# Sliding attention's queries and keys, made with channels on partitions and scored 32 rows at a time

## The chip, the cores and the metric

The kernel runs on one core of a Trainium2 chip. The metric is the device time of one execution in microseconds; of the kernel before there are three runs, and one further execution with the hardware profiler on. Lower is better.

## What is computed

A trunk of two layers over one sequence of 256 tokens with 1024 channels. Each layer normalises its input, multiplies it by one wide matrix `w_in` (1024 by 12,832 columns), and cuts the product into the inputs of three token mixers and of their gates: a state-space scan (branch A), sliding-window attention (branch B) and forgetting attention (branch C). The three results are projected, weighted by sigmoid gates, summed, projected once more and added to the stream. The change is in branch B:

```
q = rope(q.reshape(b, s, 16, 64), cos, sin)      # 16 query heads of 64 channels
k = rope(k.reshape(b, s, 4, 64), cos, sin)       # 4 key heads, each for 4 query heads
scores = einsum('bnqkgd,bnskd->bnkgqs', qb, kb) * 64 ** -0.5
# a query sees itself and the 127 tokens before it; each head has a sink logit
probs = softmax(concat([masked scores, sink]))[..., :-1]
out = einsum('bnkgqs,bnskd->bnqkgd', probs, vb) * silu(z)

def rope(x, cos, sin):                            # x1, x2: channels 0..31 and 32..63 of a head
    return concatenate([x1 * c - x2 * s, x2 * c + x1 * s], axis=-1)
```

All values are float32.

## The kernel before

*Products.* A float32 product with weights is made of three products in the type `F32R`: weights and activations are split into a high part and a low rest, and high times high, low times high and high times low are accumulated. Weights come from HBM in pieces of 256 to 512 columns, each cut into parts of 1024 values per partition (`load_part`, DMAs on SP's queue, six buffers). ACT writes a part's high half, DVE its low half (`split`, L258 to L265; `feed`, L353), at most four parts ahead of their use (`AHEAD`), into six buffers. A piece takes 8 blocks of contraction times 3 terms = 24 products for each of two halves. There are two forms. `tok` (L445) has tokens on partitions: 128 tokens are stationary, the piece's columns are the moving operand, once for each block t of 128 tokens. `chan` (L438) has channels on partitions: 128 columns of the piece are stationary, all 256 tokens move. Products stream their moving operand "in turn" (columns i and n/2 + i alternating); the pieces of 272 columns alone are streamed in plain order (`turn=False`).

*Branch B, before.* Queries and keys are made by `tok`. `rope` (L463) multiplies the product by the cosine and sine rows with three DVE instructions, POOL adds the two results (L495, L519), then PE transposes them by the identity (L101) and ACT writes the transposed blocks out (L490, L503, L528): 2 transposes for each block of queries (`u_bq`), 4 for each block of keys (`u_bkv`). So a head's 64 channels lie on one half of the partitions, and two heads stand on top of each other. `swa_quad` scores a group of four heads: 8 products that contract 64 rows, two heads side by side on the two row halves, into four PSUM tiles of their own. Products like these are in plain float32, and each leaves two records in the trace.

*The quad.* `attn_quad` (L534) is shared with forgetting attention: scores on PE, a fused add and minimum on DVE (L561), exponentials on ACT (L567), scaling on DVE (L579), 12 transposes on PE, evictions on ACT (L596), products with the values on PE.

*What sets the order.* PE's order is written out by the program. The heavy work is a list of operations (`ops`), each one half of a piece. Between two of them `pump` enters waiting pieces of the light work (quads, scan groups, norms, transposes) when their due time has come on a clock that adds up estimated costs of PE instructions; a generator's `yield D_...` is the time until its next part is due, a yielded name or condition holds it until a token or a state is there. `drain` forces what is left. On DVE, ACT and POOL a scheduler orders by priority, but in the first stage of layer 0 the program's order stands there as well.

*Layer 0's start.* To begin early, the first pieces are multiplied with activations that aren't normalised, and the products are scaled by 1/rms afterwards (`y.rn`, for rope by scaled tables, L1306). In the meantime `normalize` (L1164) spreads 1/rms over partitions by two products with `ones`, scales the transposed activations (L1178, four DVE instructions) and splits them again. Channel-form products can come only after that. Before, this stage holds keys, values, all queries, the step sizes of the scan (`C_DT`, in a piece of 272 columns with queries) and a value piece of branch C (352 columns); those of branch C were cut to 352, 344 and 344 columns and hold its forget logits too.

*Layer 1's start.* The normalised activations of token block 0 are there earlier than those of block 1, so the first operations are in token form on block 0: keys and values as one piece of 512, and queries of 256.

Of the kernel before, what the change touches and what calls it, by code (L numbers as in the profile page):

```python
# [44 lines left out]
def hybrid_trunk(  # L45
# [45 lines left out]
    def mm(o, a, b, **kw):  # L91
        n = b.free_size()
        if a.dtype == F32R:
            clock["t"] += max(0.094, n / 2350.0)
        else:
            clock["t"] += max(0.2, n / 587.0) * (0.5 if a.free_size() == 64 else 1.0)
        nc.tensor.matmul(o, a, b, **kw)  # L97
# [90 lines left out]
    rope_sb = T("rope", [P, 2, 2, 64])  # L188
# [113 lines left out]

    subs = []
# [91 lines left out]
    def load_rope(queue):  # L395
        queue.dma_start(rope_sb, rope_tab.rearrange("(t p) c d -> p t c d", p=P))

    def layer_consts(y, queue):
        l = y.l
        pdma = pin(queue.dma_start)  # L400
        if l:
            load_rope(queue)
# [60 lines left out]
    def rope(y, p, t):  # L463

        p4 = p.rearrange("p a (h d) -> p a h d", h=2)
        a = T("L1", [P, 4, 64])
        b = T("L1", [P, 4, 64])
        a4, b4 = (v.rearrange("p (a h) d -> p a h d", a=2) for v in (a, b))
        for o, i, r in ((a4, p4, rope_sb[:, t, 0, :]),
                        (b4[:, :, :, 0:32], p4[:, :, :, 32:64], rope_sb[:, t, 1, 0:32]),  # L470
                        (b4[:, :, :, 32:64], p4[:, :, :, 0:32], rope_sb[:, t, 1, 32:64])):
            tt(o, i, bc(bc(r, 1, 2), 1, 2), op=ALU.mult)
        return a, b

    def u_bkv(y, c0, t, placed=None):


        def f(w):
            p = tok(y.hTh, y.hTl, w, t) if placed is None else ordered(placed[t][:, 0:w.n])
            if t == 0 and c0 == 0:  # L480
                kv = T("L8", [P, 2048])
                y.kT = kv[:, 0:1024].rearrange("p (h s) -> p h s", h=4)
                y.bv = kv[:, 1024:1536].rearrange("p (t c) -> p t c", t=2)
            (late.append if placed is not None else lambda g: g())(lambda: evict(w, p))

        def evict(w, p):
            if c0 > 0:
                act(halves(y.bv[:, t, :]), p, AF.Copy, scale=y.rn[:, t:t + 1])
            elif w.n == 512:
                act(y.bv[:, t, :], p[:, 1, :], AF.Copy)  # L490
            if c0 == 0:
                a, b = rope(y, p if w.n == 256 else halves(p[:, 0, :]), t)
                kd = T("L2", [P, 4, 2, 64])
                for i in range(2):
                    gtt(kd[:, :, i, :], a, b, op=ALU.add)  # L495
                launch(1, rest(kd), D_K if y.rn is None else 2 * D_K)
            pump()

        def rest(kd):
            pt = pmx()  # L500
            for h in range(4):
                transpose(pt[:, h * P:(h + 1) * P], kd[:, h, :, :].rearrange("p a b -> p (a b)"), ident)
            act(y.kT[:, :, t * P:(t + 1) * P], pt.rearrange("p (h s) -> p h s", h=4), AF.Copy)  # L503
            yield 0.0
        return f

    def u_bq(y, c0, t, mid=None):

        def f(w):
            p = tok(y.hTh, y.hTl, w, t, turn=w.n != 272, mid=mid)  # L510
            if w.n == 272:
                logits(y, t, 0, p[:, 0:16])
                p = halves(p[:, 16:272])
            for i in range(w.n // 256):
                if t == 0:
                    y.qT[c0 + i] = T("qt", [P, 2, S])
# [345 lines left out]
    def fox_quad(y, j):  # L862
# [17 lines left out]
        def scored():  # L880
            tokens["bias"] += 1
# [468 lines left out]
```

## Time and profile before

| | |
|---|---|
| median of 3 runs (lowest, highest) | 839.42 us (839.38, 839.81) |
| the profiled execution's own time | 839.45 us |
| its span, first to last instruction | 837.7 us |
| granted TensorE clock, mean | 0.999 |
| HBM read, written | 154.76 MB, 2.16 MB |
| instructions | 16280 |

The page of the profile gives busy times of the engines (PE is TensorE's products, PEld its weight loads, DVE VectorE, ACT ScalarE, POOL GpSimd, SP the queue that issues the weights), the span in 40 slices, the chain of work that ended last, and groups of instructions. A group's name is what it writes, an arrow, and what it reads: `mm<-L,hi` is a product into PSUM tile `mm` with activations `L` moving over stationary weights `hi`. Rows of a group end with a count, the busy time, the mean length in ns, and the idle time ahead of it with its cause.

### The profile page before, as it was taken

To read this page: it belongs to the slowest core of one execution; us is meant where nothing else is said; L and a number is where in the kernel's file an instruction comes from. 1 tells how busy PE (TensorE), PEld (TensorE's weight loads), DVE (VectorE), ACT (ScalarE), POOL (GpSimd) and SP (SyncE) were. 2 spreads that over 40 slices of the span, in tenths; PEclk is the share of its full clock that TensorE was granted. 3 is DMA by queue.
4 is the path that set the end of the run, shared out by engine and by line. 5 is a ranking of instruction groups with operands and counts; after the bars stand their busy time and mean duration, and the time that the engine had idled before them with its cause. 6 is when DMAs were issued, how large, how long until landed. Compare 5 with 4: busy or idle time off the path is not lost.

```text
span 837.7 us, 16280 instructions
## 1 busy us (share of the span) xinstructions
PE 828.7 (99%) x6067; PEld 767.2 (92%) x6067; DVE 650.2 (78%) x1426; ACT 510.9 (61%) x1022; POOL 102.3 (12%) x141
## 2 busy tenths in 40 slices
PE   8999999999999999999999999999999999999996
PEld 8999999989999998888999999999899999988896
DVE  6987898998766679665787688899968667785665
ACT  7477768665666657443654676876557567654442
POOL 1810000000221010220024000100003110121000
PEclk9999999999999999999999999999999999999999
DMA  9775467676565556665676544765756564476632
GB/s 307 220 216 169 119 185 229 204 214 203 153 198 176 153 165 203 207 221 186 211 247 213 152 121 147 226 216 187 247 175 183 155 189 151 153 238 214 214 101 76
DMA packets 123113, 157.99 MB, mean 189 GB/s; under 512 B 5746, under 2 KB 90090, under 8 KB 123034
## 3 DMA queue, kind: packets, MB, share of 16 engines
q1 hardware_dynamic: 108816, 140.53, 53.6%
q10 hardware_dynamic: 13962, 16.37, 6.2%
q8 instruction: 48, 0.79, 0.4%
q14 instruction: 31, 0.25, 0.1%
q0 software_dynamic: 256, 0.05, 0.0%
HBM read 154.76 MB, written 2.16 MB: 187 GB/s over the span
## 4 chain that ended last, share of the span: by engine, by line
PE 98%; DMA 1%; DVE 0%; SPq 0%; POOLq 0%; issue 0%; ACT 0%
PE mm L97 84%; PE mx L97 9%; PE mx L101 4%; DMA L<-in_x_dram 1%; SPq L330 0%; SPq L164 0%; DVE L L1214 0%; POOLq L1346 0%; ACT L L1028 0%; DVE L L1222 0%; DVE L L1003 0%; DVE L L1007 0%; DVE sm L230 0%; DVE rs L232 0%; DVE sm L256 0%
## 5 line engine op out<-in xcount | busy, mean ns | idle before, releaser
L262 DVE TENSOR_TENSOR lo<-raw,hi 128x1024 fp32r<-128x1024 f32 (+3 forms) x262 | 312.7, 1208 | 85.8 <-ACT hi L261 75.4
L97 PE MATMUL mm<-hi,L 128*128 128x512 f32 (+4 forms) x1424 | 376.5, 352 | 0.2
L97 PE MATMUL mm<-L,hi 128*128 128x256 f32 x1792 | 318.0, 279 | 0.0
L261 ACT ACTIVATE hi<-raw 128x1024 fp32r<-128x1024 f32 (+3 forms) x262 | 264.1, 1022 | 84.7 <-PE mm L97 76.6
L97 PEld LDWEIGHTS mm<-L,hi 128*128 128x128 f32 x1792 | 277.9, 192 | 7.4 <-issue 3.9
L97 PEld LDWEIGHTS mm<-hi,L 128*128 128x128 f32 x1424 | 251.0, 190 | 26.3 <-issue 2.1
L97 PE MATMUL mm<-lo,L 128*128 128x512 f32 (+4 forms) x712 | 247.1, 348 | 0.0
L97 PE MATMUL mm<-L,lo 128*128 128x256 f32 x896 | 246.7, 275 | 0.0
L97 PEld LDWEIGHTS mm<-L,lo 128*128 128x128 f32 x896 | 172.1, 192 | 0.2
L97 PEld LDWEIGHTS mm<-lo,L 128*128 128x128 f32 x712 | 134.6, 190 | 12.3
L874 POOL TENSOR_SCALAR_AFFINE_SELECT bias<-bias 128x128 f32<-128x128 f32 x64 | 34.1, 569 | 409.5 <-DMA bias<-cumd 291.1
L567 ACT ACTIVATE pp<-pp,nm 128x128 f32<-128x128 f32 (+1 forms) x128 | 56.6, 444 | 13.2 <-DVE nm L561 11.2
L696 DVE SCALAR_TENSOR_TENSOR L<-L,vec,L 128x255 f32<-128x255 f32 (+2 forms) x96 | 46.1, 481 | 2.1 <-ACT L L693 1.1
L699 ACT ACTIVATE L<-L 128x256 f32<-128x256 f32 x32 | 13.3, 417 | 41.1 <-DVE L L696 41.1
L898 ACT ACTIVATE L<-L 128x512 f32<-128x512 f32 x24 | 15.2, 631 | 36.5 <-DVE L L897 36.3
L97 PE MATMUL mx<-L,L 128*64 128x128 f32 (+1 forms) x384 | 34.5, 314 | 0.0
L579 DVE TENSOR_SCALAR pp<-pp,rsum 128x128 f32<-128x128 f32 (+1 forms) x128 | 32.3, 317 | 0.3
L780 ACT ACTIVATE L<-mm 128x256 f32<-128x256 f32 x48 | 18.1, 378 | 20.5 <-PE mm L97 20.5
L97 PEld LDWEIGHTS mx<-L,L 128*64 128x64 f32 x384 | 22.9, 136 | 8.3 <-issue 1.4
L596 ACT ACTIVATE L<-mx 128x512 f32<-128x512 f32 x48 | 26.8, 596 | 1.2 <-PE mx L101 1.0
L101 PE MATMUL mx<-ident,pp 128*128 128x128 f32 x192 | 26.3, 273 | 0.0
L897 DVE TENSOR_TENSOR L<-mm,L 128x512 f32<-128x512 f32 x24 | 16.5, 687 | 12.3 <-PE mm L97 12.3
(187 smaller groups left out, 726.6 us busy)
## 6 DMA issues: line engine op xcount, KB each, us to landing
raw<-in_w_in_dram SPq DMA_DIRECT2D x179, 512.0 KB, 4.6
raw<-in_w_proj_dram SPq DMA_DIRECT2D x48, 512.0 KB, 4.5
raw<-in_w_out_dram SPq DMA_DIRECT2D x16, 512.0 KB, 4.8
raw<-in_w_in_dram SPq DMA_DIRECT2D x16, 344.0 KB, 3.2
L<-cumd ACTq DMA_DIRECT2D x8, 512.0 KB, 5.0
bias<-cumd ACTq DMA_DIRECT2D x16, 256.0 KB, 3.6
L<-in_gate_bias_dram ACTq DMA_DIRECT2D x12, 256.0 KB, 5.2
raw<-in_w_in_dram SPq DMA_DIRECT2D x8, 352.0 KB, 3.3
```

Source lines behind the costliest of these rows:

```text
L97: nc.tensor.matmul(o, a, b, **kw)
L101: nc.tensor.transpose(o, a, i)
L261: keep(act)(hi, src, AF.Copy)
L262: keep(tt)(lo, src, hi.bitcast(F32), op=ALU.subtract)
L567: act(pp[:, i, sl], pp[:, i, sl], AF.Exp, scale=-1.0, bias=nm[:, e:e + 1], accum_out=sums[:, e:e + 1])
L579: ts(pp[:, i, sl], pp[:, i, sl], rs[:, 2 * i + b:2 * i + b + 1], 0.5, op0=ALU.mult, op1=ALU.mult)
L596: act(pT, pt, AF.Copy)
L696: stt(a[:, s:S], x_[:, 0:S - s], y.vec[:, 16 * j + u:16 * j + u + 1], a[:, s:S], op0=ALU.mult, op1=ALU.add)
L780: act(halves(th), p, AF.Tanh, scale=0.5)
L874: nc.gpsimd.affine_select(out=bias[:, i, dst], in_=bias[:, i, src], compare_op=ALU.is_ge, fill=NEG, base=0, pattern=[[-1, P]], channel_mul ...
L897: tt(halves(g), p, halves(y.gb), op=ALU.add)
L898: act(g, g, AF.Tanh, scale=0.5)
```

## The change

- Queries and keys are made by `chan`, so they come out with channels on partitions, and nothing is transposed. Their weights' columns are reordered when they are split: of four heads, the first 32 channels of each fill the first 128 columns, the other 32 the second (`turned`, in `feed`). The split of such a part is two instructions on each engine instead of one.
- The cosine and sine tables are turned once by PE at the start (`tables`, two transposes, eight ACT copies). Each half of the product is multiplied by both on DVE (`rotated`), and POOL adds and subtracts (`add_rotated`).
- A head's two channel halves lie on the same 32 rows. The keys, made once, are shifted by 32, 64 and 96 rows with six SBUF-to-SBUF DMAs from POOL's queue, so that each query head finds its key head on its own row quarter.
- Scores are 16 products of 32 rows: for each query block and each channel half, four heads on the four row quarters, accumulated over the two channel halves.
- The pieces' order and widths change. Layer 0 starts with values and two 256-column value pieces of branch C; layer 1 with branch C's values (512) and the values. Then keys and four query groups in channel form. The step sizes and the forget logits move into two pieces of 272 columns with branch C's values, which are streamed in turn; the decay logits follow the second.
- The first sliding quad waits for the first gate piece in layer 0 too; the values lie in a `bias` buffer.

```diff
@@ mm @@
-            clock["t"] += max(0.2, n / 587.0) * (0.5 if a.free_size() == 64 else 1.0)
+            clock["t"] += max(0.2, n / 587.0) * (0.5 if a.free_size() == 64 or a.shape[0] == 32 else 1.0)
@@ feed @@
-            split(hi, lo, raw, keep=pin if state["pin"] else lambda f: f)
+            keep = pin if state["pin"] else lambda f: f
+            if stream[state["split"] - 1][0] in turned:
+                for c in range(2):
+                    split(*(v[:, :, c * P:(c + 1) * P].rearrange("p k (h e) -> p k h e", h=4) for v in (hi, lo)),
+                          raw.rearrange("p k (h c e) -> p c k h e", h=4, c=2)[:, c, :, :, :], keep=keep)
+            else:
+                split(hi, lo, raw, keep=keep)
@@ queries and keys @@
-    def rope(y, p, t):
...
-    def u_bkv(y, c0, t, placed=None):
...
-    def u_bq(y, c0, t, mid=None):
...
+    def rotated(y, done):
+
+        held = {}
+
+        def u(half):
+            def f(w):
+                p = chan(y, w, half * P)
+                for i in (half, 1 - half):
+                    m = held[half, i] = T("L1", [P, S])
+                    tt(halves(m), p, halves(cs[:, i, :]), op=ALU.mult)
+                if half == 1:
+                    done(held)
+                pump()
+            return f
+        return u(0), u(1)
+
+    def add_rotated(o, held):
+
+        gtt(o[:, 0, :], held[0, 0], held[1, 1], op=ALU.subtract)
+        gtt(o[:, 1, :], held[1, 0], held[0, 1], op=ALU.add)
+
+    def u_bk(y):
+
+        def done(held):
+            y.kT = T("L8", [P, 4, 2, S])
+            add_rotated(y.kT[:, 0, :, :], held)
+            for d in range(1, 4):
+                m = 32 * d
+                nc.gpsimd.dma_start(y.kT[m:P, d, :, :], y.kT[0:P - m, 0, :, :])
+                nc.gpsimd.dma_start(y.kT[0:m, d, :, :], y.kT[P - m:P, 0, :, :])
+        return rotated(y, done)
+
+    def u_bq(y, g):
+
+        def done(held):
+            q = T("qt", [P, 2, S])
+            add_rotated(q, held)
+            launch(1, swa_quad(y, g, q), D_Q)
+        return rotated(y, done)
@@ scores, now handed to attn_quad @@
-        for p in range(2):
-            for b in range(2):
-                for i in range(2):
-                    r = slice(64 * i, 64 * i + 64)
-                    mm(score(p, i, b), qTs[p][r, b * P:(b + 1) * P], kTs[p][r, 0:(b + 1) * P],
-                       start=True, stop=True)
+        products(score)
@@ swa_quad @@
-        yield lambda: (1, 0) in y.zdone or (y.l == 0 and y.rn is None)
+        yield lambda: (1, 0) in y.zdone
+
+        def products(score):
+            for b in range(2):
+                for c in range(2):
+                    for h in range(4):
+                        r = slice(32 * h, 32 * h + 32)
+                        mm(score(h // 2, h % 2, b), q[r, c, b * P:(b + 1) * P], y.kT[r, (h - g) % 4, c, 0:(b + 1) * P],
+                           start=(c == 0), stop=(c == 1))
@@ order of the pieces @@
         if l == 0:
-            k, v = cols(C_BK), cols(C_BV)
-            op(k, *(u_bkv(y, 0, t, first) for t in range(2)))
-            op(v, *(u_bkv(y, 256, t) for t in range(2)))
+            v, cv0, cv1 = cols(C_BV), cols(C_CV), cols(C_CV + 256)
+            op(v, *(u_bv(y, t, first) for t in range(2)))
             op(None, lambda: layer_consts(y0, nc.gpsimd))
-            for c, n in ((1, 512), (3, 256)):
-                op(cols(C_BQ + 256 * c, n), u_bq(y, c, 0), u_bq(y, c, 1))
-            op(None, lambda y=y: layer_vec(y))
-            op(cols(C_DT, 272), u_bq(y, 0, 0), u_bq(y, 0, 1))
             op(None, lambda: launch(9, normalize(y0), 0.0))
-            cv(0, 352)
+            op(cv0, u_cv(y, 0, 0), u_cv(y, 0, 1))
+            op(cv1, u_cv(y, 256, 0), u_cv(y, 256, 1))
+            op(None, lambda: tables(fin["rope"]))
             op(None, lambda: normalized(y0))
         else:
-            kv, q3 = cols(C_BK, 512), cols(C_BQ + 768)
+            cv0, v = cols(C_CV, 512), cols(C_BV)
             op(None, lambda: drain(5))
-            op(kv, u_bkv(y, 0, 0))
-            op(q3, u_bq(y, 3, 0, pump))
+            op(cv0, u_cv(y, 0, 0))
+            op(v, u_bv(y, 0))
             op(None, lambda: drain(6))
-            op(kv, u_bkv(y, 0, 1))
-            op(q3, u_bq(y, 3, 1))
-            op(None, lambda y=y: layer_vec(y))
-            op(cols(C_DT, 272), u_bq(y, 0, 0), u_bq(y, 0, 1))
-            op(cols(C_BQ + 256, 512), u_bq(y, 1, 0), u_bq(y, 1, 1))
-        zs(C_ZB, 1)
+            op(cv0, u_cv(y, 0, 1))
+            op(v, u_bv(y, 1))
+        op(rcols(C_BK), *u_bk(y))
+        for g in range(4):
+            op(rcols(C_BQ + 256 * g), *u_bq(y, g))
+        op(None, lambda y=y: layer_vec(y))
+        for b in range(3):
+            z1(C_ZB, 1, b)
...
-            lights = {1: [lambda: cv(696, 344)], 3: [lambda: cv(352, 344)], 5: ...
+            lights = {0: [lambda: z1(C_ZB, 1, 3)], 1: [lambda: cv(512, 0)], 3: [lambda: cv(768, 1)], 5: ...
...
-            lights = {0: [lambda: cv(696, 344)], 2: [lambda: cv(0, 352)], 3: [lambda: cv(352, 344)],
+            lights = {0: [lambda: z1(C_ZB, 1, 3)], 1: [lambda: cv(512, 0)], 3: [lambda: cv(768, 1)],
@@ tables @@
+    def tables(rope_sb):
+        p = pmx()
+        for t in range(2):
+            transpose(p[:, t * P:(t + 1) * P], rope_sb[:, t, :, :].rearrange("p c d -> p (c d)"), ident)
+        for i, src in ((0, slice(0, 32)), (1, slice(96, 128))):
+            for r in range(4):
+                act(cs[32 * r:32 * r + 32, i, :], p[src, 0:S], AF.Copy)
```

In layer 0 the branch C pieces are 256, 256, 272 and 272 columns, in layer 1 512, 272 and 272; `lights` names the operations that follow a given convolution piece.

More of the change, by code (lines that the diff above doesn't have):

```diff
@@ L297, in dense2 @@
                         release(w, k // w.kper + 1)
+    turned = set()
     subs = []
@@ L1290, in hybrid_trunk @@
         hl(1, 4)
-        for k in (0, 2):
-            w_high(parts[2], k)
-            w_low(parts[2], k)
+        for i in range(2):
+            w_high(parts[2], i)
+            w_low(parts[2], i)
         square(1, 0)
@@ L1300, in hybrid_trunk @@
         r0 = root(v, 2)
-        for k in (0, 2):
-            w_high(parts[3], k)
-            w_low(parts[3], k)
+        for part in parts[3:]:
+            for i in range(2):
+                w_high(part, i)
+                w_low(part, i)
         y0.rn = rsqrt(v, 2, r0)
-        for t in range(2):
-            ts(rope_sb[:, t, :, :], rope_sb[:, t, :, :], y0.rn[:, t:t + 1], None, op0=ALU.mult)
         for i, f, _ in ops[:2]:
```

164 lines of the change are left out of this document (62 added, 102 removed).

## Prediction

> **What bounds the kernel now.** First the page: engines, slices, chain.
>
> ```profile
> span 837.7 us, 16280 instructions
> PE 828.7 (99%) x6067; PEld 767.2 (92%) x6067; DVE 650.2 (78%) x1426; ACT 510.9 (61%) x1022; POOL 102.3 (12%) x141
> ...
> PE   8999999999999999999999999999999999999996
> ...
> PEclk9999999999999999999999999999999999999999
> ...
> PE 98%; DMA 1%; DVE 0%; SPq 0%; POOLq 0%; issue 0%; ACT 0%
> ```
>
> TensorE is busy in all slices but the first and the last at the full granted clock, and 98% of the chain that ended last is TensorE's own work. A busy share can hide waits, so the waits of PE and the busy times by stage come next.
>
> ```profile
> PE mx L101 <- POOL ident masks.py:199: 1.5, 1, 1.5
> PE mx L101 <- DMA L<-in_x_dram: 0.5, 1, 0.5
> ```
>
> ```profile
> 16.00:56.00 40.00, 40.00 (x291) 38.41 (x289) 35.67 (x67) 24.01 (x41) 21.04 (x25) 1.00 0.76 227
> 56.00:230.00 174.00, 174.00 (x1383) 162.08 (x1382) 153.34 (x385) 119.30 (x267) 8.05 (x9) 1.00 0.61 187
> ```
>
> PE waits for others twice, 2.0 us in all, both before the first product. From 16 us on (first pair of numbers: length of the stretch, PE busy) it isn't idle at all, in the stage that the change rebuilds (16 to 230 us, and its twin in layer 1) least of all. So the end moves by what the change does to PE's stream of instructions, plus any wait that it brings. Next: what one instruction of that stream costs. A group's mean is a matmul's length with its pipeline, which overlaps the next one's:
>
> ```profile
> L97 PE MATMUL mm<-L,lo 128*128 128x256 f32 x896 | 246.7, 275 | 0.0
> ```
>
> The price in a full stream is read from the chain instead, whose pieces are start, length and count.
>
> ```profile
> 31.62 0.87 PE mx L101 x8
> ```
>
> ```profile
> 32.49 5.36 PE mm L97 x48
> ...
> 41.95 3.01 PE mm L97 x24
> ...
> 49.64 1.79 PE mm L97 x12
> ```
>
> ```profile
> 72.99 5.36 PE mm L97 x48
> 78.35 1.51 PE mx L97 x16
> 79.86 2.88 PE mm L97 x24
> ...
> 116.12 1.75 PE mm L97 x12
> ```
>
> ```profile
> 327.24 49.21 PE mm L97 x228
> ```
>
> By the order of the program these are: 48 products with 256 moving columns, 5.36/48 = 0.1117 us each; 24 with 272, 0.1254; 12 with 352, 0.149; 12 with 344, 0.1458; 228 with 512, 0.2158; 8 transposes of 128 columns, 0.109 each. From 344 to 512 a column costs 0.42 ns, with only some 0.003 us per product beside the columns; 256 is dearer per column (0.1117 for 0.107 on that line). So cutting wide products into narrow ones costs little, though not nothing.
>
> The piece of 16 at 78.35 is one sliding quad's scores. It takes 1.51, and the 24 products after it take 2.88 in place of 24 x 0.1117 = 2.68: one quad costs 1.71 us.
>
> **The change, part by part.** The durations are of the profiled execution: 839.45 us, of which the span is 837.7 and 1.75 lie around it; the median of the runs shown is 839.42, so the sum can be set against either.
>
> (1) *Transposes go.* Queries: 2 for each of 4 column blocks, 2 token blocks and 2 layers, 32; keys: 4 x 2 x 2 = 16. The new tables add 2. So 46 fewer at 0.109: -5.0 us. They stand in PE's stream without a wait before or after, so all of it is on the path.
>
> (2) *Other widths.* Same columns in all, 192 more products. A piece of weights of any width takes 48 (8 blocks of the contraction, 3 split terms, 2 halves); there are ten more pieces of 256 columns, two fewer of 512, four fewer of 344, two fewer of 352, two more of 272: +480, -96, -192, -96 and +96 products. Without the 272s: 480 x 0.1117 - 96 x 0.2158 - 192 x 0.1458 - 96 x 0.149 = 53.6 - 20.7 - 28.0 - 14.3 = -9.4. The 272s are 96 now and 192 then. Now their weights are streamed in plain order (the one `turn=False`), and 0.1254 is dear for the width; then they are streamed in turn, as the 256s and 344s are, and the line between these gives 0.1179. 192 x 0.1179 - 96 x 0.1254 = +10.6. Sum: +1.2 us. If they stay at 0.1254 it is +2.6; on the steeper-starting line from 344 and 512 (0.1158), +0.8. I take the value in turn, since the moving operand's order is what the neighbours share.
>
> (3) *Scores.* Per quad 8 products of 64 rows become 16 of 32 rows, four heads side by side, two contractions one after the other. No row shows 32-row products, so the price is bounded.
>
> ```profile
> 155.44 0.88 PE mx L97 x6
> ```
>
> ```profile
> L97 PE MATMUL mx<-L,qt 64*128 64x128 f32 x64 | 7.0, 297 | 0.0
> L97 PE MATMUL mx<-L,bt 128*128 128x256 f32 x16 | 4.8, 380 | 0.0
> ```
>
> An f32 product leaves two records (8 quads x 4 products of 128 columns are 64 records; 8 of `bt` are 16). The piece at 155.44 is one `bt` product of 256 columns and two of 128, one after the other: 0.88 us for 512 columns, 1.72 ns a column. A quad's 1536 columns would take 2.64 us at that price, but 1.71 were paid: 1.32 for two heads at once at full speed, and 0.39 for going into and out of that mode. After: 3072 columns per quad, one head at a time 5.3 + 0.4 us, two at once 2.64 + 0.39 = 3.03, four at once 1.32 + 0.39 = 1.71. Over 8 quads: +32 us, +10.6 us, or 0. On the other side nothing but the 0.39 could be saved, at most 3 us. Nearest is the row of the two row halves: these run side by side with no loss, into separate PSUM tiles, and the four quarters have four tiles as well. I take 0 and keep -3 to +10.6; one at a time contradicts the quad's row and is left out.
>
> (4) *Start of layer 0.* Today the normalised activations are wanted after keys, values, all queries and a value piece; in the changed order, two pieces of 256 columns after the values. The products on PE that open it (`ones`, 0.45 us) and the DVE work behind them:
>
> ```profile
> 49.19 0.45 PE mx L97 x4
> ```
>
> ```profile
> 12.73 1.29 DVE L1230 TENSOR_TENSOR lo<-raw,hi 128x512 fp32r<-128x512 f32 x2
> ...
> 17.89 0.16 DVE L211 TENSOR_TENSOR rs<-sm,sm 128x2 f32<-128x2 f32 x1
> 18.09 0.48 DVE L1306 TENSOR_SCALAR rope<-rope,rs 128x128 f32<-128x128 f32 x2
> 18.48 2.35 DVE L262 TENSOR_TENSOR lo<-raw,hi 128x1024 fp32r<-128x1024 f32 x2
> 20.76 0.82 DVE L472 TENSOR_TENSOR L<-mx,rope 128x256 f32<-128x256 f32 x3
> ...
> 49.68 2.48 DVE L1178 TENSOR_TENSOR L<-L,mx 128x512 f32<-128x512 f32 x4 [0.83 <-PE mx L97]
> 52.07 2.49 DVE L262 TENSOR_TENSOR L<-L,L 128x512 fp32r<-128x512 f32 x4
> ```
>
> ```profile
> 15.73 0.39 PE L97 MATMUL mm<-hi,L 128*128 128x256 f32 x2
> ```
>
> PE is through with the first 256 columns at 15.73. Then two pieces of 5.36, the 0.45 and two transposes: the first normalised product is due at 27.1, the second half of the activations 12 products later, at 28.5. DVE is free at 18.1 (rope's scaling is gone), splits two parts of weights (2 x 1.2, to 20.5), and has four half parts of the keys' weights queued ahead of the normalising (4 x 0.64, to 23.1); then 8 x 0.62 and one more half part: 28.7. The halves must be there in this order, so PE waits a few tenths; I take 0.4 us, from 0 (all fits) to 2 (a weight part lands late: the DMA share is 0.91 there).
>
> ```profile
> 0.00:16.00 16.00, 13.56 (x88) 12.18 (x89) 9.24 (x18) 10.55 (x22) 2.44 (x15) 1.00 0.91 307
> ```
>
> (5) *What I cost at nothing.* DVE: rope's 20 triples (0.82 each) go and 40 multiplications of 128x256 come (at 0.4, with the start), about even; splitting keys' and queries' weights in halves adds an instruction's start 20 times. ACT loses 20 evictions of transposes, and gets 8 small copies and 20 more splits. Cover: DVE has 20 us idle between 56 and 230 us, and the splits run up to four parts ahead, some 10 us of PE's work; without it each late split would be PE's wait. POOL: two additions per group, and in each layer six SBUF-to-SBUF transfers that bring the keys to the other quarters.
>
> ```profile
> L495 POOL TENSOR_TENSOR L<-L,L 128x256 f32<-128x256 f32 x8 | 9.6, 1227 | 14.8 <-DVE L L472 11.0 <-ACT L L261 3.8
> L256 POOL DMA_DIRECT2D vr<-in_conv_w_dram x1 | 0.8, 802 | 0.0
> ```
>
> ```profile
> raw<-in_w_in_dram SPq DMA_DIRECT2D x179, 512.0 KB, 4.6
> ```
>
> After the keys: 2 x 1.2 of adding, 6 x 0.8 of issuing, and 5 us to land are 12 us. Behind them on POOL only the queries' additions are queued. The first score comes four groups (21.4 us) and one gate half (2.7) later, so 12 us are left over; only past that would PE wait.
>
> Sum: -5.0 + 1.2 + 0 + 0.4 = -3.4: 839.45 - 3.4 = **836.0 us**.
>
> **Rivals.** *Only two row groups at once* (place: the eight sliding quads; it decides as soon as the third quarter has to wait for the first): +10.6 us, 846.6, slower. For it: no row shows more than two at once. Against: the halves lose nothing beside each other, and 0.39 of 1.71 us is mode, not contention. *The mode costs twice*: 32-row sets pay the 0.39 on top again, 8 x 0.39 = +3.1, 839.1, no difference. The Trainium skill has such a loss: in "TensorE: Matmul & The Clock Gate", Part 3 (Packing small matmuls), four row tiles with 32 rows and 512 columns are measured at 3.07 times one, not 4. By that ratio, as an estimate, the 1.32 us become 1.72, the same +3 us; the two halves of this trace show no such loss. *A new wait*: PE has none now, and the order after is another one. Layer 1's sliding quads begin only after all queries, the decay logits come behind the fourth convolution piece in place of the second (layer 0) and first (layer 1), and scan groups and forgetting quads stand closer. One wait for DVE of a split's length or two (1.2 to 2.4 us) at two places of each layer gives +3 to +6 us: 839 to 842. For it: DVE is at 88% between 56 and 230 us. Against: the same spacing rules place the groups. That the transposes stay is excluded: the order of PE's instructions has 46 fewer.
>
> **How the numbers follow.** Forecast 0.52 (836.0, own range 834.8 to 837.7); new wait 0.20, half of it within the bound of no difference; mode twice 0.13; two at once 0.15. A measurement of this kernel can tell about 0.2% (1.7 us) from no change. Faster: 0.52. Same: 0.13 + 0.10 = 0.23. Slower: 0.15 + 0.10 = 0.25. The range runs from 834.8 (the 272s at 0.1158, no wait at the start) to 847, the end of the unknown score price.
>
> **What would show it.** The chain after: a sliding quad's scores as 32 records in 1.5 us, and the products behind them at 2.88 for 24 (3); pieces of 5.36 for 48 through keys and queries, without transposes between (1); 272s near 0.118 (2); PE's waits still 2 us, with at most a small new one on the normalised activations near 27 us (4). Scores of 2.8 us per quad would show two at once. A busy sum on PE below this one's and a span that isn't shorter would show a wait that I haven't seen.

## Result and the profile after

The changed kernel takes 849.03 us (median of 4 runs, 847.47 to 849.31) against 839.41 us for the kernel before on the same chip (4 runs, 839.38 to 839.81): a ratio of 1.011, 95% interval 1.0092 to 1.0127. The forecast was 836.0 us, with a range of 834.8 to 847. The profiled execution took 849.02 us, with a span of 847.3. First the page of after, the lines that answer to those of before:

```profile
span 847.3 us, 16833 instructions
PE 829.6 (98%) x6341; PEld 766.5 (90%) x6341; DVE 652.4 (77%) x1418; ACT 509.0 (60%) x1030; POOL 94.5 (11%) x149
...
PE   8999999999999999999999999997999999999996
...
PEclk9999999999999999999999999998999999999999
...
PE 80%; DVE 10%; ACT 4%; DMA 3%; issue 2%; POOL 0%; SPq 0%; ACTq 0%; POOLq 0%; DVEq 0%
```

Busy sums of all engines are those of before within 3 us (POOL's is 8 us smaller). What changed is the chain: 98% PE became 80%, and one slice of PE's row, near 570 us, dips to 7, with a dip of the granted clock behind it. A busy sum can't show this. The waits of PE can (total, times, longest):

```profile
PE mm L97 <- DVE L L262: 4.6, 1, 4.6
PE mx L101 <- POOL ident masks.py:199: 1.5, 1, 1.5
PE mm L97 <- ACT L L683: 1.1, 1, 1.1
PE mx L97 <- DVE da L650: 1.1, 2, 0.6
PE mm L97 <- ACT L L261: 0.7, 1, 0.7
...
PE mm L97 <- DVE lo L262: 0.2, 1, 0.2
```

Of these lines only the one with `ident` was there before. By stage (length, then busy times of PE, PEld, DVE, ACT, POOL, and PEclk, DMA share, GB/s):

```profile
16.00:56.00 40.00, 40.00 (x358) 39.80 (x357) 36.96 (x62) 27.31 (x52) 17.52 (x25) 1.00 0.93 274
56.00:230.00 174.00, 173.08 (x1455) 160.08 (x1454) 147.92 (x374) 115.41 (x261) 9.19 (x21) 1.00 0.62 184
...
560.00:580.00 20.00, 13.61 (x96) 11.62 (x95) 13.84 (x34) 10.91 (x23) 2.55 (x8) 0.96 0.64 200
580.00:590.00 10.00, 10.00 (x41) 8.43 (x41) 8.41 (x12) 4.80 (x7) 0.00 (x0) 0.75 0.71 219
```

The rebuilt start of layer 0 has no idle time. The loss stands in layer 1, from 560 to 590 us: 6.4 us of idle PE, then products at a lowered clock. The chain of waits there leads back to a broadcast:

```profile
558.51 8.73 DMA L<-cumd
...
567.26 0.04 DVE ds L714
...
578.46 0.61 DVE L L262
...
579.12 6.87 PE mm L97 x17
```

and DVE's instructions in order of time show how it works (the bracket is idle time ahead of an instruction and what ended it):

```profile
560.65 0.16 DVE L714 TENSOR_TENSOR ds<-L,acum 128x4 f32<-128x4 f32 x1
560.73 1.00 DVE L686 SCALAR_TENSOR_TENSOR L<-L,vec,L 128x255 f32<-128x255 f32 x2
567.26 0.17 DVE L714 TENSOR_TENSOR ds<-L,acum 128x4 f32<-128x4 f32 x1 [5.54 <-DMA L<-cumd]
567.35 0.48 DVE L686 SCALAR_TENSOR_TENSOR L<-L,vec,L 128x253 f32<-128x253 f32 x1
567.74 1.22 DVE L262 TENSOR_TENSOR lo<-raw,hi 128x1024 fp32r<-128x1024 f32 x1
...
572.64 0.68 DVE L590 TENSOR_TENSOR L<-mx,L 128x512 f32<-128x512 f32 x1
...
578.38 0.68 DVE L262 TENSOR_TENSOR L<-L,L 128x512 fp32r<-128x512 f32 x1
```

The second scan group's first step, `ds`, needs the cumulated decays broadcast to all partitions by a DMA (`L<-cumd`). DVE reached it 3.2 us after the broadcast's issue (558.51) and stood at it for 5.54 us; PE was busy all that time. Behind it in the queue were convolution steps, weight splits and the scan's own steps. The sliding branch's gated output was written at 572.64 (L590), but its split into high and low part came only at 578.38, behind more of these steps, and PE waited 4.6 us for it, while DVE was busy. In all, DVE waited for these broadcasts 10.3 us, longest 5.5:

```profile
DVE ds L714 <- DMA L<-cumd: 10.3, 4, 5.5
```

In the kernel before the same wait is 3.3 us, longest 2.2:

```profile
DVE ds L724 <- DMA L<-cumd: 3.3, 3, 2.2
```

PE's idle times behind 16 us sum to 8.6 us. Read in windows of 1 us, the granted clock is 0.50 from 579 to 585 us, which costs some 3 us: together 11.6 of the 13.0 us that lie between the result and the forecast. The other 1.4 us are not assigned.

### The profile page after: what moved, and what is told of

Its sections match the earlier page's. It is cut to its first block, busy times and chain, and to the rows that moved or that the text cites. A ratio compares the mean times of both kernels' runs of the same rounds, so it can differ in the third digit from the quotient of the medians.

```text
span 847.3 us, 16833 instructions
## 1 busy us (share of the span) xinstructions
PE 829.6 (98%) x6341; PEld 766.5 (90%) x6341; DVE 652.4 (77%) x1418; ACT 509.0 (60%) x1030; POOL 94.5 (11%) x149
## 4 chain that ended last, share of the span: by engine, by line
PE 80%; DVE 10%; ACT 4%; DMA 3%; issue 2%; POOL 0%; SPq 0%; ACTq 0%; POOLq 0%; DVEq 0%
PE mm L97 70%; PE mx L97 7%; DVE lo L262 3%; PE mx L101 3%; DMA L<-cumd 2%; ACT hi L261 2%; DMA L<-in_x_dram 1%; DVE L L686 1%; ACT pp L548 1%; DVE L L724 1%; DMA cumd<-L 0%; DVE pp L542 0%; DVE pp L560 0%; DVE L L690 0%; DVE L L262 0%
## 5 line engine op out<-in xcount | busy, mean ns | idle before, releaser
L262 DVE TENSOR_TENSOR lo<-raw,hi 128x1024 fp32r<-128x1024 f32 (+2 forms) x276 | 315.6, 1159 | 84.2 <-ACT hi L261 77.9
L97 PE MATMUL mm<-L,hi 128*128 128x256 f32 x2112 | 371.5, 278 | 0.0
L97 PE MATMUL mm<-hi,L 128*128 128x512 f32 (+2 forms) x1232 | 326.7, 354 | 6.7 <-DVE L L262 4.6
L97 PEld LDWEIGHTS mm<-L,hi 128*128 128x128 f32 x2112 | 326.3, 192 | 7.3 <-issue 3.9
L261 ACT ACTIVATE hi<-raw 128x1024 fp32r<-128x1024 f32 (+2 forms) x276 | 266.1, 981 | 107.9 <-PE mm L97 91.2
L97 PE MATMUL mm<-L,lo 128*128 128x256 f32 x1056 | 290.4, 275 | 0.0
L97 PEld LDWEIGHTS mm<-hi,L 128*128 128x128 f32 x1232 | 218.1, 191 | 32.1 <-DVE L L262 5.2
L97 PE MATMUL mm<-lo,L 128*128 128x512 f32 (+2 forms) x616 | 215.0, 351 | 0.2 <-DVE lo L262 0.2
L97 PEld LDWEIGHTS mm<-L,lo 128*128 128x128 f32 x1056 | 202.6, 192 | 0.1
L542 DVE CUSTOM_DVE_ANT_0 pp<-mx,wmask,nsink 128x128 f32<-128x128 f32 x64 | 23.9, 412 | 1.4 <-PE mx L97 1.4
L894 DVE TENSOR_TENSOR L<-mm,L 128x512 f32<-128x512 f32 x24 | 16.5, 686 | 9.7 <-PE mm L97 9.7
```

The costliest lines, as they stand in the source:

```text
L261: keep(act)(hi, src, AF.Copy)
L262: keep(tt)(lo, src, hi.bitcast(F32), op=ALU.subtract)
L542: nc.vector.tensor_tensor_reduce(out=pp[:, i, sl], in0=score(p, i, b), in1=biases(p, i, b), scale=-0.125, scalar=1.0e30 if ns is None else ...
L894: tt(halves(g), p, halves(y.gb), op=ALU.add)
```

## Experiments

All times are medians. Each ratio, with its interval, is to runs of the kernel before on the same chip as the run; the row of before puts these together. "Waits" are PE's idle times behind 16 us in the profiled execution. E4, E8a, E8b and E16 are edits of the kernel before, all others of the changed kernel.

| run | us (lowest, highest) | ratio to before, 95% interval | waits, us |
|---|---|---|---|
| before | 839.6 (838.8, 840.5) | | 0.0 |
| after | 849.03 (847.47, 849.31) | 1.011 (1.0092, 1.0127) | 8.6 |
| E1 logits early | 855.11 (854.74, 856.34) | 1.0186 (1.0172, 1.02) | 12.8 |
| E2 the same, layer 1 only | 850.82 (850.05, 851.67) | 1.0133 (1.0119, 1.0147) | 10.2 |
| E3 pause | 847.39 (846.58, 848.73) | 1.0093 (1.008, 1.0107) | 9.2 |
| E4 before, logits late | 845.36 (843.83, 846.16) | 1.0061 (1.0048, 1.0075) | 3.4 |
| E5 heads in turn | 851.14 (849.0, 852.5) | 1.0135 (1.0122, 1.0148) | 10.7 |
| E6 quads early | 847.47 (846.96, 849.34) | 1.0096 (1.0083, 1.0109) | 7.8 |
| E7 quads and logits early | 850.13 (849.26, 850.87) | 1.0123 (1.011, 1.0136) | 8.5 |
| E8a before, quads late | 839.3 (838.61, 839.9) | 0.9995 (0.9987, 1.0004) | 0.1 |
| E8b before, both late | 842.61 (841.48, 845.39) | 1.0042 (1.0028, 1.0057) | 2.1 |
| E9 logits first | 844.07 (843.82, 845.46) | 1.0056 (1.0043, 1.0069) | 4.6 |
| E10 tie | 842.46 (841.86, 843.63) | 1.0037 (1.0025, 1.0049) | 5.0 |
| E11 E9's order, tie | 841.96 (839.7, 843.74) | 1.0025 (1.0014, 1.0036) | 3.9 |
| E12 E11, two short pauses | 839.65 (839.3, 840.49) | 1.0001 (0.9992, 1.001) | 3.1 |
| E13 E12, high priority | 840.04 (839.02, 841.22) | 1.0005 (0.9996, 1.0014) | 3.1 |
| E14 E11, no pause | 838.59 (837.99, 840.02) | 0.999 (0.9981, 0.9998) | 2.1 |
| **E15 tie in the changed order** | **836.79 (836.41, 837.92)** | **0.9968 (0.9956, 0.9981)** | **1.1** |
| E16 before, tied | 840.33 (839.32, 841.25) | 1.0008 (0.9999, 1.0017) | 0.6 |
| E17 E15, sums later | 841.84 (840.55, 843.43) | 1.0028 (1.0016, 1.0039) | 4.6 |

### First theory: the decay logits come too late (E1 to E4)

E1 moves the two pieces with the decay logits forward, in both layers; E2 in layer 1 alone:

```diff
-lights = {0: [lambda: z1(C_ZB, 1, 3)], 1: [lambda: cv(512, 0)], 3: [lambda: cv(768, 1)], ...
+lights = {0: [lambda: cv(512, 0)], 1: [lambda: cv(768, 1)], 3: [lambda: z1(C_ZB, 1, 3)], ...
```

> The changed kernel with the two value pieces that carry the decay logits behind the first and the second convolution piece of each layer, and the gate piece that stood there behind the fourth; the same instructions, only moved. Theory (the loss is a wait: the decay sums come so late that the two scan groups' broadcasts of them land while VectorE's queue already stands at them, and the weight splits behind come late): VectorE's wait for the broadcasts falls from 10.3 us in all to under 4, TensorE's waits from some 10 us to about 2, the run to 836 us (834.5 to 838), ratio 0.996. Rival A (the rotated keys and queries, their products or the weight splits in halves cost it on VectorE or TensorE): the waits move but stay, 845 to 849 us. Rival B (the wait only moves, since a broadcast is slow behind the weight loads wherever it is issued): 840 to 845 us, VectorE's wait still over 6 us.

> The same move in layer 1 alone; layer 0 as in the changed kernel. Theory: layer 1 holds the five-microsecond stall and the half clock behind it, some 11 of the 13 us; so 837 to 839 us, with layer 0's short waits of about 2.5 us left. If the loss is spread over both layers: about 842 to 843 us. Rival A: 847 to 849 us.

Both missed, on the wrong side, and DVE's waits for the broadcasts didn't fall in E1 (11.8 us for 10.3). PE's waits in E1:

```profile
PE mm L97 <- DVE L L262: 4.7, 2, 4.4
PE mm L97 <- DVE L L773: 4.0, 2, 2.1
...
PE mm L97 <- DVE lo L262: 1.4, 1, 1.4
```

The logits, now due earlier, were entered ahead of the last sliding quad: its scores began at 550.8 us in place of 537.3, so its gated output was split late again, and new waits came in front. So moving the logits alone doesn't remove the loss. The broadcast stayed in the chain:

```profile
538.96 5.64 DMA L<-cumd
...
584.67 0.61 DVE L L262
```

E3 leaves the order and puts a pause between a group's broadcast and its work:

```diff
         nc.scalar.dma_start(bcg, y.cumd[4 * g:4 * g + 4, 0, :].partition_broadcast(P))
+        yield 8.0
```

> The changed kernel with its late decay logits, but with a pause of 8 us of the schedule between the issue of a scan group's broadcast and the group's first work on it (all eight groups): the broadcast is as late as before, only nothing is queued on VectorE that waits for it. Theory (what costs is the wait in VectorE's in-order queue, not the lateness itself): TensorE's stall of 4.9 us near 574 us and the half clock behind it go, the short waits for the decay steps (da) stay at 1 to 2 us; 837 to 840 us. Rival C (the late scan groups delay the gated outputs and the projections, whatever queue they stand in): 846 us or more, with TensorE's waits moved to the scan's own products or to the split of the gated output.

The pause did not do what it was meant to. The wait on DVE is still there, 8.5 us behind the broadcast's issue at 561.90 (8.7 in after):

```profile
570.43 0.16 DVE L715 TENSOR_TENSOR ds<-L,acum 128x4 f32<-128x4 f32 x1 [5.32 <-DMA L<-cumd]
```

A `yield` moves what PE does, since PE's order is that of the program. DVE's is made by the scheduler, and `ds`, which needs nothing from PE, was drawn ahead of the pause. PE's long wait went even so: its waits for such a split are 0.9 us at most, with no half clock behind them. Shorter waits came in its place, 9.2 us in all, and the time fell by 1.6 us only. It lies in the range of rival C, but since DVE still stood at the broadcast, E3 doesn't decide between rival and theory. E4 makes the logits late in the kernel before (the pieces of 344 columns trade places):

```diff
-lights = {1: [lambda: cv(696, 344)], 3: [lambda: cv(352, 344)], ...
+lights = {1: [lambda: cv(352, 344)], 3: [lambda: cv(696, 344)], ...
```

> The kernel before, with nothing of the queries and keys changed, but with the value piece that carries the forgetting logits behind the fourth convolution piece in both layers, as in the changed kernel, and the piece that stood there in its old place. Theory: this order alone makes waits; VectorE waits for the broadcasts 8 us or more in all (3.3 now) and TensorE 4 to 12 us; 844 to 852 us. Rival A (the queries' and keys' new form is the cause, by its load on VectorE): 839 to 841 us.

The time is as expected in sign and size: 5.6 us, without any change to queries and keys. The waits are smaller than expected: DVE waits 6.3 us for the broadcasts (8 or more forecast), PE 3.4 us (4 to 12). One broadcast on the chain took twice the 5.0 us of its median in the profile of before:

```profile
560.36 10.75 DMA L<-cumd
```

### Second theory: the quads come too late (E6 to E9)

In layer 1 a value piece and the keys now stand ahead of the queries. E6 lets the quads begin 10 us earlier; E7 adds E1's move:

```diff
         for g in range(4):
             op(rcols(C_BQ + 256 * g), *u_bq(y, g))
-        op(None, lambda y=y: layer_vec(y))
-        for b in range(3):
+            if g == 1:
+                op(None, lambda y=y: layer_vec(y))
+                z1(C_ZB, 1, 0)
+        for b in (1, 2):
```

> The changed kernel with its first gate piece (for which the sliding quads wait before their first scores) moved from behind the fourth query group to behind the second, in both layers; the decay logits stay late. Theory 2 (in layer 1 the value piece of 512 columns and the keys now stand ahead of the queries, so the four quads run some 10 us later against the projection that needs their output, and the scan groups, which wait until no sliding quad is open, crowd VectorE's queue just ahead of it): the quads' scores start 10 us earlier, the last of layer 1 near 527 us, TensorE's wait of 4.6 us for the split of the gated output and the half clock behind it go; 837 to 841 us. Theory 1 (only the decay logits' place counts; which the first move of them contradicts): no gain, 847 to 850. Rival B (the broadcasts' landing alone): the split's wait stays at 4 us or more, 845 to 849.

> Both moves: the first gate piece behind the second query group, and the decay logits behind the first and second convolution piece. Theory 2: with the quads early the decay logits no longer push the last quad back, so this is the order with the fewest waits: 835 to 838 us, faster than before. Rival (VectorE and ScalarE have no room for logits and quads in the same stretch whatever the order): 842 us or more, with waits of TensorE between 110 and 150 us and their twin in layer 1, as in the first move of the logits.

The quads did start early (the last of layer 1 at 527.9 us in E6), the wait for the gated split went, and yet 8 us were lost. In E6 DVE still stands at the broadcast for 5.2 us, ACT's `ds` waits for DVE's, and an eviction (L683) for which PE waits 4.8 us stands behind it:

```profile
569.15 0.20 ACT L715 ACTIVATE ds<-ds 128x4 f32<-128x4 f32 x1 [5.78 <-DVE ds L714]
```

In E7 nearly the whole loss is one wait in each layer, for a PSUM tile, with some 6 us more lost to half clock behind the two: the decay sums' products follow the fourth quad's scores, whose tiles the softmax still holds. And the first quad is now near enough to the keys' shift to wait for its DMA:

```profile
PE mx L97 <- DVE nm L542: 7.8, 2, 3.9
...
PE mx L97 <- DMA L<-L: 0.7, 1, 0.7
```

The counterparts in the kernel before hold layer 1's quads two gate pieces longer (E8a), and with E4's edit (E8b):

```diff
-        yield lambda: (1, 0) in y.zdone or (y.l == 0 and y.rn is None)
+        yield lambda: (1, 4) in y.zdone or (y.l == 0 and y.rn is None)
```

> The kernel before, where the sliding quads of layer 1 are held until the third gate piece in place of the first (two pieces, 10.7 us later); all else, the early decay logits too, as before. Theory 2: this alone brings a wait of some us ahead of the projection of the sliding branch in layer 1: 843 to 848 us. If the quads' lateness costs nothing without the rotated form: 839 to 840 us.

> The kernel before with both: layer 1's sliding quads held two gate pieces longer, and the logits piece behind the fourth convolution piece in both layers. If the order is the whole cause, this loses what the changed kernel loses beside its savings of 3.4 to 3.8 us on TensorE: 849 to 854 us, with a wait of TensorE of about 5 us and half clock behind it near 575 us. If the late decay logits alone are the cause, no more than with these alone: 844 to 847 us. If the new form of the queries and keys is, 839 to 841 us.

E8a costs nothing: in the kernel before, late quads alone make no wait, and in the changed one (E6) early quads gain 1.6 us only. So the second theory falls as the account of the loss. E8b costs 3 us, less than E4 alone and in none of the three ranges; what an order costs is not a sum of its parts. E9 puts both logits pieces first (`lights` 0: `cv(512, 0)`, `cv(768, 1)`; 1: the gate piece), on E6:

> The changed kernel with the first gate piece behind the second query group and both logits pieces behind the first convolution piece (the last gate piece behind the second): against the run with both moves, the decay sums' products now stand ahead of the fourth quad's scores on TensorE and not right behind them, where they waited twice 4.1 us for a PSUM tile that the softmax of that quad held. Theory 3 (TensorE's own stream is as long as forecast, 835 to 837 us of span in every version; what each version adds are the waits of its own order, 8 to 13 us with the half clock behind the long ones): if no new long wait arises, 837 to 840 us, the 4.1 us waits gone. Rival (the rotated form itself slows the stream): the waits go and the time stays above 845.

The PSUM waits went as expected, and new ones came (2.1 us behind `DVE L L894`): 844, not 837 to 840. Six orders of the changed kernel (after, E1, E2, E6, E7, E9) all take 844 us or more, and what they lose stands mostly in PE's waits: without the idle time behind 16 us, and with the stretches at half clock taken at full clock, their spans are 834.6 to 836.9 us, against 837.7 before. That is near the 835 to 837 of theory 3.

### The wait itself: tying the scan's work to TensorE (E10)

E10 keeps the changed kernel's order. The steps that read the broadcast now also read a copy of the sums that is written behind the group's transposes, so the scheduler can't draw them ahead of these; the pause of E3 lies before:

```diff
         nc.scalar.dma_start(bcg, ...)
+        yield 8.0
...
+        acg = T("acg", [P, 2, 4], bufs=2)
+        act(acg.rearrange("p c h -> p (c h)"), p[:, 0:8], AF.Copy)
+        act(acg, y.acum[:, :, hs], AF.Copy)
         ds = T("ds", [P, 4], bufs=2)
-        tt(ds, bcg[:, :, P - 1], y.acum[:, 0, hs], op=ALU.subtract)
+        tt(ds, bcg[:, :, P - 1], acg[:, 0, :], op=ALU.subtract)
... dec reads acg[:, c, h:h + 1]; cx is first written with a copy of acg
```

> The changed kernel, order of the pieces untouched; but the scan group's work on the broadcast (ds, the decay factors, cx) reads a copy of the sums that is made behind the group's transposes on TensorE, 8 us of the schedule after the broadcast is issued, so that the scheduler can't put it into VectorE's and ScalarE's queues ahead of that point, as it did in spite of the pause alone. Three small ScalarE copies per group come on top. Theory 1 in its narrow form (VectorE and ScalarE stand in order at the broadcast, and what is behind comes late): VectorE's waits for the broadcast fall from 10.3 us to under 3, the 4.9 us wait near 574 us and its half clock go, the waits for da (1.4 us) stay: 838 to 842 us. Rival (VectorE's backlog, not the wait in it, is what makes the gated output late): the wait near 574 us stays at 3 us or more, 846 to 850.

The mechanism holds: no wait of DVE for a broadcast is left, and the wait of 4.6 us and the half clock near 580 us are gone. The time, 842.5, is half a us above the forecast range. What is left is a wait for the last group's normalisation (L809) in each layer, with some half clock behind the first, and the old `da`. The L809 waits come with the long pauses: E3 (at L805 there) and E11 below have them too, E12 and E14 don't.

```profile
PE mx L97 <- ACT L L809: 2.9, 2, 1.4
...
PE mx L97 <- DVE da L650: 1.1, 2, 0.6
```

### Tied, with less pause (E11 to E17)

E11 is E10's edit on E9's order. E12 cuts the pause to 5.0 and to groups 0 and 1; E13 adds `with tc.high_priority():` around the decay logits' vector steps; E14 has the tie and no pause; E15 is E13's edit on the changed kernel's own order.

> Both: the order of pieces of the run with the logits behind the first convolution piece, and the scan's work tied behind its transposes. Theory 3 with theory 1: the fewest waits of all, 836 to 838.5 us, no slower than before. Rival: a new wait of 3 us or more elsewhere, 843 or more.

> The same without the high priority. If the priority is what matters, the da waits of 0.5 us in each layer stay and this is 1 us slower than its neighbour; 836.5 to 839 us.

> The run with both (logits behind the first convolution piece, the scan's work tied behind its transposes), with the pause cut to 5 us of the schedule and only in the first two scan groups of a layer, and the decay logits' vector steps given high priority. The two waits of 1.6 us for the last scan group's normalisation near 318 and 730 us, and the half clock behind them, came from the pauses of four groups; the two of 0.5 us for da from the steps' place in VectorE's queue. If the waits are the whole difference, this has almost none: 835.5 to 838 us, ratio 0.995 to 0.998. If the freed groups collide elsewhere: 840 to 844.

> The same tie behind the transposes, with no pause at all. If the tie alone is enough (the scheduler's hoisting was the fault), VectorE's wait for the broadcasts stays under 4 us and the time is 836 to 839; if the broadcast's 5 to 8 us of landing need the pause, the wait is 8 us or more and the time 842 to 848.

> The changed kernel's own order of pieces (gate piece behind the fourth query group, decay logits late), with the tie, the two pauses of 5 us and the high priority. If the broadcast in the in-order queues was the changed kernel's whole loss: 836.5 to 839.5 us. If the late quads and logits cost something of their own: 841 to 845, with waits left between 545 and 580 us.

E11 missed: 842.0, between its forecast and its rival, with the L809 waits of E10. The priority makes no difference in that order (E13 against E12; the `da` waits stayed at 0.7), and the tie alone is enough there (E14). E12 and E13 kept a wait of 1.8 us that their expectation hadn't; E12 came out just above its range, E13 at the lower end of its rival's. E15, at the low end of its range, answers whether the reader of the broadcast was the whole loss: nearly, since 12.2 of the 13.0 us come back in the changed kernel's own order. Its page and PE's waits:

```profile
span 834.8 us, 16840 instructions
PE 824.9 (99%) x6341; PEld 765.5 (92%) x6341; DVE 653.8 (78%) x1418; ACT 511.4 (61%) x1054; POOL 99.1 (12%) x149
```

```profile
PE mx L101 <- POOL ident masks.py:199: 1.5, 1, 1.5
PE mx L97 <- DVE da L651: 1.1, 2, 0.6
PE mx L101 <- DMA L<-in_x_dram: 0.3, 1, 0.3
```

Same pieces in the same order as the changed kernel, 12.2 us faster, and 0.3% faster than before. E16 puts the same edit into the kernel before, as a control (one buffer for `acg`):

> A control: the kernel before, with nothing of the queries and keys changed, with the same tie of the scan's work behind its transposes, the two pauses and the high priority of the decay logits (one buffer for the copy of the sums, for space). Before has no wait on TensorE after its start, so there is nothing for the tie to win: 839 to 841 us, and the changed kernel with the tie is then 0.3% faster by its shorter stream alone. If the tie is a gain of its own, whatever the change, 835.5 to 837.5 us, and the change's own gain would be near nothing.

840.3: the tie wins nothing where nothing waits, so E15's gain over the kernel before is the change's. E17 moves E15's decay sums later (`D_CUM` 14.5 in place of 12.0):

> The tied changed kernel with the decay sums' products 2.5 us of the schedule later (14.5 in place of 12): the last two waits of TensorE (0.6 us for da in each layer) go. If nothing else moves, 835.3 to 836.5 us, some 1 us faster than the tied one; if the sums, broadcasts and the last quad collide, 838 to 842.

The time is in the range of its second case. The `da` waits went and three others came; the small shift cost more than it saved:

```profile
PE mx L97 <- ACT L L577: 1.6, 1, 1.6
...
PE mm L97 <- ACT L L261: 1.5, 1, 1.5
PE mm L97 <- DVE L L262: 1.3, 2, 1.0
```

### The scores by themselves (E5)

E5 exchanges the loops `c` and `h` in `swa_quad`, so that the two contractions of a head follow each other:

> The changed kernel with the loops of the sliding scores exchanged: the two 32-row contractions of one head one right after the other, and the four heads in turn; the same 16 products per quad. If the row quarters run side by side only when neighbours in the queue are on different quarters, a quad's scores go from 1.5 us to 3 to 5 us: 8 quads, +12 to +30 us, 861 to 880, unless waits nearby give some back. If the hardware overlaps them whatever the order, or never did, no difference: 849.

Neither: a quad's 32 records take 1.64 us,

```profile
471.30 1.64 PE mx L97 x32
```

0.12 more than in the changed order (below), 1 us over 8 quads. The profiled execution is 3.5 us longer than after's (852.50 against 849.02), and another 2.1 of these are waits. Row quarters overlap in this order almost as well.

## Why the prediction was wrong

The steps on TensorE were right; what failed is (5), the work and waits of the other engines, put at nothing. The chain of after has the pieces:

```profile
26.91 26.80 PE mm L97 x240
...
78.82 1.52 PE mx L97 x32
80.34 2.88 PE mm L97 x24
...
114.51 5.58 PE mm L97 x48
```

- *(1) Transposes go, -5.0:* right; the keys and the four query groups are one piece of 240 products, 5 x 5.36 us, without transposes between them.
- *(2) Other widths, +1.2:* 48 products of 272 columns take 5.58, 0.1163 each (0.1179 forecast): 192 x 0.1163 - 96 x 0.1254 = 10.3, so +0.9.
- *(3) Scores, 0 from a range of -3 to +10.6:* 1.52, and 0.20 at the 24 products behind (2.88 for 2.68): 1.72 per quad for 1.71. Four row quarters run at once at the price of two halves; the rivals of two groups at once and of a mode that costs twice are out. The ratio of 3.07 of the Trainium skill ("TensorE: Matmul & The Clock Gate", Part 3), on which the latter drew, is not what these products show.
- *(4) Start of layer 0, +0.4:* no idle time between 16 and 56 us, so 0 in place of 0.4.

In E15 the span without the waits behind the start is 834.8 - 1.1 = 833.7 us, 4.0 less than before; (1) to (3) forecast 3.8. So the change does to TensorE's stream what was worked out, and with the wait removed the time is 836.8, against 836.0. Two slips of the working change nothing of this: the line from 344 and 512 columns gives 0.109 us at 256, not 0.107, and the terms named for the low end of the range give 835.2, not 834.8 (the -3 of the scores isn't in it).

- *(5) "What I cost at nothing"* failed. Its cover was "DVE has 20 us idle between 56 and 230 us, and the splits run up to four parts ahead". Idle time summed over a stage covers nothing behind an instruction that blocks an in-order queue: DVE was idle 5.54 us ahead of `ds`, and what stood behind it came later. The lead of four parts did hold, but it covers splits of weights only: PE waited 0.2 us for `lo`. The 4.6 us were for a split of activations, the sliding branch's gated output, which has no such lead.
- *The rival "a new wait"* was the case, and its place was named: "the decay logits come behind the fourth convolution piece". Its price, 3 to 6 us from waits of "a split's length or two", was too small: it left out the broadcast's landing (8.73 us here, of which DVE stood 5.54; the median on the page of before is below) and the half clock behind the wait. DVE already waited 2.2 us for a broadcast in the profile of before, where only PE's waits were read; that row could have raised the rival's price and its chance of 0.20.

```profile
L<-cumd ACTq DMA_DIRECT2D x8, 512.0 KB, 5.0
```

- *The sign for an unseen wait* (a busy sum on PE below that of before) didn't come: 829.6 us against 828.7. Some 3 us of it are products lengthened by the half clock; in E15, with the same products and no half clock, it is 824.9.

Shown: the scan's steps that wait for the broadcast, drawn early into DVE's and ACT's queues, cause the large wait (E10, E15 against after; E16 as control), and late logits alone bring such waits, though smaller, to the kernel before (E4). Not separated: the tie takes DVE's standing at the broadcast away, and it also puts the scan's steps behind the split of the gated output (written at 564.03 in E15, split at 565.91, first `ds` at 572.60). E3, where DVE stood 5.3 us and PE's long wait was gone, says that the standing alone doesn't make it. Not settled: which share of E15's last 5.7 us over E10 belongs to the shorter pauses and which to the priority, and why each moved piece loses at the place where it does. E1, E2, E6, E7, E9 and E17 each traded waits for others, which suggests that this order has little slack, not how to choose one.

## What to carry to other kernels

When a change moves work between stages, list for each DMA whose reader sits in an in-order queue when it is issued, when it lands, and what stands behind the reader; a wait of an engine off the critical path in the profile of before (here 2.2 us of DVE, which cost nothing there) shows where such a queue can start to cost. Where a scheduler orders an engine, a pause in the program doesn't hold an instruction back; a dependence on something that runs late does. And when every reordering loses at another place, look for what all of them keep, here the broadcast's reader: DVE waited 7.3 to 11.8 us for the broadcasts in all six orders.

## What the runs showed of the hardware

*Half clock can follow a wait of 1.4 us, and the length alone doesn't decide.* In the profiles of this case every wait of PE of 2.1 us or more behind the start (ten, 2.1 to 4.8 us) has products at half clock behind it. Of 22 waits between 1.0 and 2.0 us two have, in E10 and E11. E10 waits for the same step in both layers, 1.44 and 1.43 us; of two stretches of the same work, each 1.8 us behind the end of its wait, one runs at a low clock and the other doesn't (PEclk is the third number from the end):

```profile
319.70 0.78 PE L97 MATMUL mx<-L,ones 128*128 128x128 f32 x4 [1.44 <-ACT L L809]
...
733.10 0.78 PE L97 MATMUL mx<-L,ones 128*128 128x128 f32 x4 [1.43 <-ACT L L809]
```

```profile
321.50:325.00 3.50, 3.50 (x10) 2.82 (x10) 2.47 (x7) 2.56 (x5) 0.93 (x1) 0.57 0.10 36
734.90:738.40 3.50, 3.50 (x18) 3.07 (x17) 2.47 (x7) 3.00 (x6) 0.93 (x1) 1.00 0.07 28
```

The Trainium skill ("TensorE: Matmul & The Clock Gate", "Why this matters for your kernels") asks for no idle gaps over about 3 us between bursts of products; by these rows shorter ones can already be too long.

*A broadcast of 512 KB takes 5.0 us from issue to landing by the median, but its slowest cases, 8.73 us in after and 10.75 in E4, fell into stretches with much DMA traffic* (DMA share 0.92 from 558.5 to 567.3 us in after, 0.79 from 560.4 to 571.1 us in E4, against 0.61 in after from 16 us on). That the traffic slows it is likely, but no run here tried it.
